# RWKV decays, rates and gates: computed for all head pairs when the mixing begins, as float32r products, and kept in DRAM

## The chip, the core and the metric

The kernel runs on one core of a Trainium2 chip (trn2). The metric is the device time of one execution in microseconds. A core has five engines that work beside one another: TensorE (PE; its weight loads are listed apart as PEld), VectorE (DVE), ScalarE (ACT), GpSimd (POOL) and SyncE (SP), whose queue issues nearly all DMAs here. Each engine works through its own list in order, and semaphores hold an instruction back until its inputs are there.

## What is computed

One step of a decoder layer for 512 prompt tokens and 8 x 8 sample tokens, 576 columns in all (`N`), between two SwiGLU feed-forward blocks. The middle of the layer, the mixing, has three branches (RWKV-7 time mixing, a convolution, a cross-attention), merged with gates. The change concerns these lines of the time mixing:

```
z = h @ p['w_in']
...
xm = zs + (prev - zs) * p['mu_shift']
...
r, k, v = xm[..., :c1], xm[..., c1:c2], xm[..., c2:c3]
wd, ad, gd = xm[..., c3:c4], xm[..., c4:c5], xm[..., c5:]      # widths 64, 64, 160
w_log = -jax.nn.softplus(-(p['w0'] + jnp.tanh(wd) @ p['w_decay_up'])) - 0.5
decay = jnp.exp(-jnp.exp(w_log))
a = jax.nn.sigmoid(p['a0'] + ad @ p['w_a_up'])
g = jax.nn.sigmoid(gd) @ p['w_g_up']
...
wkv_new, o = _wkv7_scan(wkv0, r_h, hd(decay), k_h, v_h, kk, kk * a_h)
...
y_a = (o.reshape(b, t, D_RWKV) * g) @ p['w_rwkv_out']
```

The decays, the rates `a` and the gates `g` have 512 channels each. They are low-rank products: 64, 64 and 160 inner channels.

## The kernel before

Channels lie on the 128 partitions and the 576 tokens in the columns, so a matrix product is a sequence of matmuls of 128 x 128 weights with 288 columns (`H`), for two halves. Large products are made in float32r: weight and operand are each split into a high part and a low part (`split`: ScalarE casts, VectorE subtracts), and three matmuls per block (high x high, high x low, low x high) are added up in PSUM (`mm3`). One projection of 128 outputs (`proj`) is 48 matmuls. Its 512 KB of weights come by DMA into one of two buffers `w` of pool `wp` (`wtile`, `wload`), and are split into the three buffers of pool `wq`. A buffer is given to the next load when its splits are done.

The mixing works on four pairs of heads (64 + 64 channels, j = 0 to 3). `lora` first makes the low-rank inputs with `shifted(12)`, `shifted(13)`, `shifted(14)`: a projection, then the token shift with `mu`. They stay in SBUF as `la` (tanh of the decay input, and the rate input) and `lg` (sigmoid of the gate input; its last 32 channels in `aux`). Then the steps of a plan written out by hand follow:

```
PLAN = ("A0 P0 I0 Y3 G0 J0 P1 B0 Y1 I1 X2 Y1 X2 J1 P2 B1 "
        "X1 I2 X2 C0 Y3 P3 J2 B2 X1 Z1 I3 Z3 J3 B3 Z2 L0 Z2")
```

A is the attention, P `prep` (operands of the chunks of pair j), I and J `inverse` and `joined` (a triangular inverse, with DMAs between), B `chain` (eight chunks in sequence, the samples, the norm and the gate of the pair), G and C the convolution, X, Y and Z output gates (projections that nothing in the pairs waits for), L the reload of the finished pairs. The order of the plan is a priority, not a fixed order: a scheduler puts each engine's list together when the program is built, by expected times, and takes later work forward where an engine would stand idle. Projections, gates and pair steps are therefore interleaved on TensorE.

In `prep` the decays and rates of a pair are products in plain float32 of `wda` (decay and rate weights, one below the other, each K = 64) with `la` (lines 805 and 819, through `full`, line 128), ScalarE applies the sigmoid, and the exponential gives `w`. In `chain` the gate is a float32 product of `wg` with `lg` (line 916, also through line 128), and VectorE multiplies the pair's result by it from PSUM (line 917).

SBUF is given out in pools that are opened and closed like a stack, from the left and from the right. When a pool comes to lie on bytes of a closed pool, all its tiles wait for every user of that pool. The first feed-forward block leaves on the left, from low to high: `x1`, `f1`, `h1`, `xe` (operands and, at its end, the memory tokens of the keys and values), `sp`. The mixing then puts `b1` and `lp` there, and, after `lora`, `b20`, `b21` and `b3`. The token-shift scratch pool `lz` lies on the right.

Of the kernel before, what the change touches and what calls it, by code (L numbers as in the profile page):

```python
# [46 lines left out]
def _q8(t, q):  # L47
    return t.rearrange("p (b q) -> p b q", q=q)


class _Builder:
# [9 lines left out]
    def par(self, name, i=0, rows=128):  # L61
        c = _COLS[name] + i
        return self.pv[:rows, c:c + 1]
# [48 lines left out]
    def proj(self, src, x, n=8, m=128):  # L112

        w = self.wload(src, n * m)
        ps = []
        for h in range(2):
            p = self.bank()[:m, :H]
            self.mm3(p, w, x, n, h, m)
            ps.append((slice(h * H, (h + 1) * H), p))
        return ps  # L120
# [47 lines left out]
    def build(self):  # L168
        tc, a = self.tc, self.a
        with ExitStack() as st:  # L170
# [14 lines left out]
            self.d_g0 = [dr.tile([128, N], F32, name=f"d_g0{i}") for i in range(8)]  # L185
            self.d_ya = [dr.tile([128, N], F32, name=f"d_ya{i}") for i in range(4)]

            s_mem = ExitStack()
# [376 lines left out]
    def shifted(self, m, out, zp):  # L565

        V, A = self.V, self.A
        rows = 32 if m == 14 else 128
        p = self.proj(self.a["w14"] if m == 14 else self.a["win"][m], self.xn, 8, rows)
# [14 lines left out]
    def lora(self, lp):  # L584
        A, a = self.A, self.a
        self.ssh = lp.tile([128, 15, NB], F32, name="ssh")
        self.sho = lp.tile([128, 15, 9], F32, name="sho")
        self.wda = lp.tile([128, 512], F32, name="wda")
        self.wg = [lp.tile([128, 512], F32, name="wg0"), lp.tile([128, 512], F32, name="wg1")[:32]]
        self.G.memset(self.sho[:, 14, :], 0.0)  # L590
        self.dma(self.ssh, a["ssh"])
        self.dma(self.wda, a["wda"])
        self.dma(self.wg[0], a["wg0"])
        self.dma(self.wg[1], a["wg1"])
        self.la = lp.tile([128, N], F32, name="la")
        aux = lp.tile([128, 600], F32, name="aux")
        self.lg = [lp.tile([128, N], F32, name="lg0"), aux[:32, :N]]
        self.t11 = aux[64:96, :N].rearrange("p (h c t) -> p h c t", h=2, c=9)
# [11 lines left out]
        for t in self.st + [self.ms, self.ax]:  # L610
            self.G.memset(t, 0.0)
        with self.tc.tile_pool(name="lz", bufs=1, side="right") as zp:
            self.shifted(12, self.la, zp)
            A.activation(self.la[:64], self.la[:64], AF.Tanh)
            for i in range(2):
                self.shifted(13 + i, self.lg[i], zp)
                A.activation(self.lg[i], self.lg[i], AF.Sigmoid)

# [172 lines left out]
    def prep(self, j):  # L791
# [6 lines left out]
        def parts(t, o=0):  # L798

            return _q8(t[:, :SEQ], 64), _q8(t[:, SEQ:N], 8)  # L800

        k, r, v = tmp("k"), tmp("r"), b2.tile([128, N], F32, name="v")

        sg = b1.tile([128, 640], F32, name="u1", bufs=2)[:, :N]
        for c, p in self.full("g", (self.wda[:64, 128 * j:128 * j + 128], self.la[:64])):
            A.activation(sg[:, c], p, AF.Sigmoid, bias=par("w0", j))
        w = b1.tile([128, PADN], F32, name="w")
        g = b1.tile([128, PADN], F32, name="g")
        for wv, sv in zip(self.padded(w), parts(sg)):
            V.memset(wv[:, :, 0:1], 0.0)  # L810
            A.activation(wv[:, :, 1:], sv, AF.Exp, scale=-0.6065306597126334)
        V.tensor_tensor_scan(g, w, self.gi, 0.0, ALU.mult, ALU.add)
# [5 lines left out]
        av = tmp("av")  # L818
        for c, p in self.full("g", (self.wda[64:, 128 * j:128 * j + 128], self.la[64:])):
            A.activation(av[:, c], p, AF.Sigmoid, bias=par("a0", j))  # L820

# [55 lines left out]
    def chain(self, j):  # L877
# [36 lines left out]
        V.tensor_tensor(rs, rs, bv, ALU.add)  # L914
        ch = slice(128 * j, 128 * j + 128)
        for c, p in self.full("c", (self.wg[0][:, ch], self.lg[0]), (self.wg[1][:, ch], self.lg[1])):
            V.tensor_tensor(rs[:, c], p, rs[:, c], ALU.mult)
        self.dbg(f"ya{j}", rs)
# [193 lines left out]
def _prep(inp):  # L1112
# [13 lines left out]
    def wt(w, cols=128):  # L1126

        K, M = w.shape
        return np.ascontiguousarray(
            w.reshape(K // 128, 128, M // cols, cols).transpose(2, 1, 0, 3).reshape(M // cols, 128, K // 128 * cols))  # L1130
# [14 lines left out]
    for i in "12":  # L1145
# [4 lines left out]
    a["win"] = wt(np.concatenate([win[:, :1792], win[:, 1824:]], axis=1))  # L1150
    a["w14"] = wt(win[:, 1792:1824], 32)[0]
    a["wya"] = wt(f["w_rwkv_out"])
    a["wcb"] = wt(f["w_conv_out"])
    a["woc"] = wt(f["w_xattn_out"])
    a["wo"] = wt(f["w_o"])
    a["wda"] = np.concatenate([f["w_decay_up"], f["w_a_up"]])
    a["wg0"] = np.ascontiguousarray(f["w_g_up"][:128])
    a["wg1"] = np.ascontiguousarray(f["w_g_up"][128:])
    cols = [vec(f["ffn1_norm"]), vec(f["mix_norm"]), vec(f["ffn2_norm"]), vec(f["final_norm"]), vec(f["mu_shift"])]
    cols += [vec(f[n].reshape(-1)) for n in ("w0", "a0", "k_k", "k_a", "r_k", "gn_g", "gn_b", "glu_b")]  # L1160
# [3 lines left out]
    a["ssh"] = np.ascontiguousarray(  # L1164
        np.concatenate([f["state_shift"], np.zeros((NB, 96), f["state_shift"].dtype)], axis=1)
        .reshape(NB, 15, 128).transpose(2, 1, 0))
# [63 lines left out]
```

## Time and profile before

| | us |
|---|---|
| median of three runs | 1486.97 (1484.86 to 1489.13) |
| the profiled execution | 1487.49 |
| its span, first to last instruction | 1485.7 |
| PE busy | 1460.2 |
| DVE busy | 1027.4 |
| ACT busy | 675.5 |
| mean granted TensorE clock | 0.982 |

How to read the rows of the profile: a group names line, engine and operation, output and inputs by the program's names (`p<-x,wh`), shapes, count; then the busy time of the group, the mean of one in ns, and the idle time of the engine just before them with what ended it. A row of the order of time begins with start and length in us. The rows of stretches give for each engine the busy time, then the granted TensorE clock, the DMA share and GB/s. A matmul's record is longer than the distance to the next one, since matmuls overlap in the array; the distance is what counts for throughput. L128 is the matmul in `full`, L110 that of `mm3k`, L96 and L97 the two halves of `split`, L86 the weight load.

### The profile page before, as it was taken

How to read it: one execution, taken by the hardware profiler on the slowest of the kernel's cores; microseconds unless marked ns; L12 is line 12 of the kernel's file. 1: busy time of each engine (PE TensorE's matmuls, PEld its weight loads, DVE VectorE, ACT ScalarE, POOL GpSimd, SP SyncE). 2: the span in 40 equal slices, each digit the busy share in tenths (PEclk: the TensorE clock that was granted, in tenths of full speed). 3: DMA queues.
4: the chain of work that ended last, by engine and by line, in shares of the span. 5: the costliest groups of instructions: out<-in, count | busy, mean ns of one | idle time of the engine just before them, and what ended most of it. 6: DMA issues, size and time to landing. Idle time of an engine off the chain costs nothing.

```text
span 1485.7 us, 27013 instructions
## 1 busy us (share of the span) xinstructions
PE 1460.2 (98%) x10778; PEld 1378.1 (93%) x10778; DVE 1027.4 (69%) x2053; ACT 675.5 (45%) x1370; POOL 4.5 (0%) x21
## 2 busy tenths in 40 slices
PE   8999999999999999999999999999999999999997
PEld 8999999999998799888889888789999999999997
DVE  7976777777784579778466456357578767777775
ACT  6443344443577535435446542444354434444342
POOL 0000000000010000000000000000000000000000
PEclk9999999999999999999899999999999999999998
DMA  6222222232632243133123134255222322322221
GB/s 209 72 84 87 86 86 86 86 98 95 205 101 86 66 132 91 46 98 96 60 65 97 55 100 126 92 177 175 100 72 72 100 73 85 102 95 89 86 86 64
DMA packets 95033, 144.04 MB, mean 97 GB/s; under 512 B 43628, under 2 KB 53228, under 8 KB 94908
## 3 DMA queue, kind: packets, MB, share of 16 engines
q1 hardware_dynamic: 94332, 141.74, 30.9%
q8 instruction: 84, 1.38, 0.4%
q10 hardware_dynamic: 576, 0.59, 0.1%
q14 instruction: 41, 0.34, 0.1%
HBM read 126.07 MB, written 16.23 MB: 96 GB/s over the span
## 4 chain that ended last, share of the span: by engine, by line
PE 92%; DVE 4%; ACT 2%; DMA 1%; issue 1%; SPq 0%; DVEq 0%; ACTq 0%
PE p L110 51%; PE p L369 26%; PE g L872 1%; PE c L1006 1%; PE c L1010 1%; PE c L1003 1%; DVE pr L965 1%; PE g L128 1%; PE c L128 1%; PE c L1038 1%; PE c L1036 1%; DMA w<-win 1%; PE p L148 1%; PE c L1021 1%; PE c L1058 1%
## 5 line engine op out<-in xcount | busy, mean ns | idle before, releaser
L110 PE MATMUL p<-x,wh 128*128 128x288 f32 x3136 | 655.4, 300 | 1.1 <-ACT kv L541 0.7
L110 PEld LDWEIGHTS p<-x,wh 128*128 128x128 f32 x3136 | 507.1, 188 | 15.2 <-issue 7.9
L110 PE MATMUL p<-x,wl 128*128 128x288 f32 x1568 | 469.7, 300 | 1.5 <-DVE wl L97 1.5
L96 ACT CAST wh<-w 128x512 fp32r<-128x512 f32 (+1 forms) x353 | 209.5, 600 | 257.2 <-PE p L110 111.9
L97 DVE TENSOR_TENSOR wl<-w,wh 128x512 fp32r<-128x512 f32 (+1 forms) x353 | 231.9, 662 | 109.2 <-ACT wh L96 102.2
L110 PEld LDWEIGHTS p<-x,wl 128*128 128x128 f32 x1568 | 295.2, 188 | 7.0 <-issue 3.1
L369 PE MATMUL p<-t,wh 128*128 128x288 f32 x1088 | 224.2, 298 | 0.0
L369 PEld LDWEIGHTS p<-t,wh 128*128 128x128 f32 x1088 | 173.8, 188 | 6.4 <-DVE t L380 6.2
L369 PE MATMUL p<-b,wh 128*128 128x288 f32 x816 | 169.7, 295 | 0.0
L369 PE MATMUL p<-t,wl 128*128 128x288 f32 x544 | 160.5, 295 | 0.0
L96 ACT CAST wh<-p 128x512 fp32r<-128x512 f32 x136 | 84.5, 621 | 155.9 <-PE p L110 117.7
L369 PEld LDWEIGHTS p<-b,wh 128*128 128x128 f32 x816 | 132.6, 188 | 0.0
L97 DVE TENSOR_TENSOR wl<-p,wh 128x512 fp32r<-128x512 f32 x136 | 93.5, 688 | 50.4 <-ACT wh L96 47.8
L369 PE MATMUL p<-b,wl 128*128 128x288 f32 x408 | 120.3, 295 | 0.0
L369 PEld LDWEIGHTS p<-t,wl 128*128 128x128 f32 x544 | 102.4, 188 | 0.0
L369 PEld LDWEIGHTS p<-b,wl 128*128 128x128 f32 x408 | 76.8, 188 | 0.0
L446 DVE SCALAR_TENSOR_TENSOR x<-p,x 128x288 f32<-128x288 f32 x128 | 57.7, 451 | 20.3 <-PE p L110 20.3
L96 ACT CAST x<-t 128x576 fp32r<-128x576 f32 (+1 forms) x60 | 36.5, 610 | 45.6 <-DVE t L450 42.3
L1030 DVE SCALAR_TENSOR_TENSOR st<-c,gc,mg 64x64 f32<-64x64 f32 x56 | 15.9, 283 | 53.3 <-PE c L1021 52.5
L359 DVE TENSOR_TENSOR p<-w 128x512 f32<-128x512 f32 x68 | 46.7, 686 | 3.2 <-DMA w<-wu 2.7
L359 DVE TENSOR_TENSOR p<-p,w 128x512 f32<-128x512 f32 x68 | 46.3, 681 | 0.1
L110 PE MATMUL p<-x,t 128*128 128x288 f32 x264 | 38.5, 306 | 5.5 <-ACT t L96 5.5
(345 smaller groups left out, 1987.8 us busy)
## 6 DMA issues: line engine op xcount, KB each, us to landing
w<-wu SPq DMA_DIRECT2D x85, 512.0 KB
w<-win SPq DMA_DIRECT2D x44, 512.0 KB
w<-wd SPq DMA_DIRECT2D x64, 256.0 KB
w<-wd SPq DMA_DIRECT2D x16, 384.0 KB
d_mb<-gate SPq DMA_DIRECT2D x16, 288.0 KB
w<-wo SPq DMA_DIRECT2D x8, 512.0 KB
x<-x SPq DMA_DIRECT2D x8, 288.0 KB
d_x<-x SPq DMA_DIRECT2D x16, 144.0 KB
```

Source lines behind the costliest of these rows:

```text
L96: self.A.copy(hi, x)
L97: self.V.tensor_tensor(lo, x, hi.bitcast(F32), ALU.subtract)
L110: self.T.matmul(p, l, x[r][:, c], start=k == 0 and i == 0, stop=k == n - 1 and i == 2)
L128: self.T.matmul(p, l, r[:, c], start=i == 0, stop=i == len(ops) - 1)
L148: self.T.matmul(p[:, o + f - d.start:o + 128 - d.start], r[f:, i], self.con("ident")[f:, f:], start=True, stop=True)
L359: V.tensor_tensor(s, u, v, ALU.add)
L369: self.T.matmul(p, hl[l][:, c], xs[k][b][:, o], start=first and k == 0 and q == 0, stop=k == 3 and q == 2, skip_group_check=True)
L446: V.scalar_tensor_tensor(x[m][:, c], p, 0.5, x[m][:, c], ALU.mult, ALU.add)
L872: T.matmul(ps[:, i * 128:(i + 1) * 128], kb[o, c + i].rearrange("p a t -> p (a t)"), ra[o, c + i].rearrange("p a t -> p (a t)"), start=Tru ...
L965: V.tensor_tensor(pr, tt[:, :n, :e].unsqueeze(2).broadcast_to([np_, n, m, e]), l3[:, t:e, :e].unsqueeze(1).broadcast_to([np_, n, m, e]), A ...
L1003: T.matmul(ps[64:, 64 * h:64 * h + 64], gr[:64, h, c, 64:], vu[:64, c, 64 * h:64 * h + 64], start=h == 0 or not inter, stop=not inter)
L1030: V.scalar_tensor_tensor(mn[s, s], ps[s, 256 + 64 * h:320 + 64 * h], gc[s, c:c + 1], mg[s, s], ALU.mult, ALU.add)
```

## The change

A new function, `low_rank`, takes the place of the three calls at the end of `lora`. It loads the decay and rate weights stacked twice (`wda`, now 128 x 1024) and the gate weights (`wg`, 128 x 1024, the last 32 rows three times) through the two buffers `w`, splits them, and makes the inputs as before, split too. High and low parts are stacked on the partitions so that a decay or rate product takes two float32r matmuls for a half, and a gate product four. Sigmoid and exponential follow for all four pairs, and `w`, `a` and the gates go to DRAM (`d_w`, `d_a`, `d_gt`). `prep` and `chain` load them back. `shifted(14)` now makes 96 rows (its 32 channels three times), and the scratch pool `lz` is on the left, above `lp`, and also holds the split weights and inputs.

```diff
     def proj(self, src, x, n=8, m=128):
-        w = self.wload(src, n * m)
+        w = self.wload(src, n * m, 512 // m * m)
...
     def shifted(self, m, out, zp):
-        rows = 32 if m == 14 else 128
+        rows = 96 if m == 14 else 128
...
     def lora(self, lp):
-        self.wda = lp.tile([128, 512], F32, name="wda")
-        self.wg = [lp.tile([128, 512], F32, name="wg0"), lp.tile([128, 512], F32, name="wg1")[:32]]
...
-        with self.tc.tile_pool(name="lz", bufs=1, side="right") as zp:
-            self.shifted(12, self.la, zp)
-            A.activation(self.la[:64], self.la[:64], AF.Tanh)
-            for i in range(2):
-                self.shifted(13 + i, self.lg[i], zp)
-                A.activation(self.lg[i], self.lg[i], AF.Sigmoid)
+        with self.tc.tile_pool(name="lz", bufs=1) as zp:
+            self.low_rank(zp)
+
+    def low_rank(self, zp):
+        two = lambda name, n: zp.tile([128, 2, n], F32R, name=name)
+        sub = lambda o, x, hi: V.tensor_tensor(o, x, hi.bitcast(F32), ALU.subtract)
+        wh, wl, gh, gl = two("wh", 512), zp.tile([128, 512], F32R, name="wl"), two("gh", 512), zp.tile(
+            [128, 512], F32R, name="gl")
+        xs, lg, gs = two("xs", N), two("lg", N), zp.tile([128, N], F32R, name="gs")
+        raw = []
+        for name in ("wda", "wg"):
+            raw.append(self.wtile())
+            self.dma(raw[-1], a[name])
+        raw = [t.rearrange("p (i c) -> p i c", i=2) for t in raw]
+        A.copy(wh, raw[0])
+        for i in range(2):
+            o = slice(64 * i, 64 * i + 64)
+            sub(wl[o], raw[0][o, i], wh[o, i])
+        A.copy(gh, raw[1])
+        sub(gl, raw[1][:, 0], gh[:, 0])
+        sub(gh[64:96, 1], raw[1][64:96, 1], gh[64:96, 1])
+
+        x = b1.tile([128, N], F32, name="k")
+        self.shifted(12, x, b1)
+        A.activation(x[:64], x[:64], AF.Tanh)
+        for i in range(2):
+            o, q = slice(64 * i, 64 * i + 64), slice(64 - 64 * i, 128 - 64 * i)
+            A.copy(xs[o, i], x[o])
+            sub(xs[q, i], x[o], xs[o, i])
+        x = b1.tile([128, N], F32, name="r")
+        self.shifted(13, x, b1)
+        A.activation(x, x, AF.Sigmoid)
+        self.split(lg[:, 0], lg[:, 1], x)
+        x = b1.tile([128, N], F32, name="av")[:96]
+        self.shifted(14, x, b1)
+        A.activation(x, x, AF.Sigmoid)
+        A.copy(gs[:96], x)
+        sub(gs[32:64], x[32:64], gs[32:64])
+
+        def products(*ops):
+            for h in range(2):
+                c = slice(h * H, (h + 1) * H)
+                p = self.bank("g")[:, :H]
+                for q, (l, r) in enumerate(ops):
+                    T.matmul(p, l, r[:, c], start=q == 0, stop=q == len(ops) - 1)
+                yield c, p
+
+        sg = [b1.tile([128, 640], F32, name="u1", bufs=2)[:, :N] for _ in range(2)]
+        sg += [b1.tile([128, N], F32, name="bv", bufs=2) for _ in range(2)]
+        for j in range(4):
+            ch = slice(128 * j, 128 * j + 128)
+            for c, p in products((wh[:, 0, ch], xs[:, 0]), (wl[:64, ch], xs[:64, 0])):
+                A.activation(sg[j][:, c], p, AF.Sigmoid, bias=self.par("w0", j))
+            t = b1.tile([128, N], F32, name=("k", "r")[j % 2])
+            for c, p in products((wh[:, 1, ch], xs[:, 1]), (wl[64:, ch], xs[64:, 1])):
+                A.activation(t[:, c], p, AF.Sigmoid, bias=self.par("a0", j))
+            self.store(self.d_a[j], t)
+        for j in range(4):
+            ch = slice(128 * j, 128 * j + 128)
+            t = b1.tile([128, N], F32, name=("av", "zt")[j % 2])
+            for c, p in products((gh[:, 0, ch], lg[:, 0]), (gh[:, 0, ch], lg[:, 1]), (gl[:, ch], lg[:, 0]),
+                                 (gh[:96, 1, ch], gs[:96])):
+                A.copy(t[:, c], p)
+            self.store(self.d_gt[j], t)
+        for j in range(4):
+            w = b1.tile([128, PADN], F32, name=("w", "g")[j % 2])
+            for wv, sv in zip(self.padded(w), (_q8(sg[j][:, :SEQ], 64), _q8(sg[j][:, SEQ:], 8))):
+                V.memset(wv[:, :, 0:1], 0.0)
+                A.activation(wv[:, :, 1:], sv, AF.Exp, scale=-0.6065306597126334)
+            self.store(self.d_w[j], w)
...
     def prep(self, j):
-        for c, p in self.full("g", (self.wda[:64, 128 * j:128 * j + 128], self.la[:64])):
-            A.activation(sg[:, c], p, AF.Sigmoid, bias=par("w0", j))
...
-        for wv, sv in zip(self.padded(w), parts(sg)):
-            V.memset(wv[:, :, 0:1], 0.0)
-            A.activation(wv[:, :, 1:], sv, AF.Exp, scale=-0.6065306597126334)
+        self.dma(w, self.d_w[j])
...
-        for c, p in self.full("g", (self.wda[64:, 128 * j:128 * j + 128], self.la[64:])):
-            A.activation(av[:, c], p, AF.Sigmoid, bias=par("a0", j))
+        self.dma(av, self.d_a[j])
...
     def chain(self, j):
-        for c, p in self.full("c", (self.wg[0][:, ch], self.lg[0]), (self.wg[1][:, ch], self.lg[1])):
-            V.tensor_tensor(rs[:, c], p, rs[:, c], ALU.mult)
+        gt = b3.tile([128, N], F32, name="gt")
+        self.dma(gt, self.d_gt[j])
+        V.tensor_tensor(rs, gt, rs, ALU.mult)
```

The host side stacks the weights, `mu_shift` and the shift state accordingly.

More of the change, by code (lines that the diff above doesn't have):

```diff
@@ L186, in build @@
             self.d_ya = [dr.tile([128, N], F32, name=f"d_ya{i}") for i in range(4)]
+            self.d_w = [dr.tile([128, PADN], F32, name=f"d_w{i}") for i in range(4)]
+            self.d_a = [dr.tile([128, N], F32, name=f"d_a{i}") for i in range(4)]
+            self.d_gt = [dr.tile([128, N], F32, name=f"d_gt{i}") for i in range(4)]
             s_mem = ExitStack()
@@ L584, in lora @@
     def lora(self, lp):
-        A, a = self.A, self.a
+        a = self.a
         self.ssh = lp.tile([128, 15, NB], F32, name="ssh")
         self.sho = lp.tile([128, 15, 9], F32, name="sho")
-        self.wda = lp.tile([128, 512], F32, name="wda")
-        self.wg = [lp.tile([128, 512], F32, name="wg0"), lp.tile([128, 512], F32, name="wg1")[:32]]
         self.G.memset(self.sho[:, 14, :], 0.0)
         self.dma(self.ssh, a["ssh"])
[L592 to L595, printed above, removed]
         aux = lp.tile([128, 600], F32, name="aux")
-        self.lg = [lp.tile([128, N], F32, name="lg0"), aux[:32, :N]]
         self.t11 = aux[64:96, :N].rearrange("p (h c t) -> p h c t", h=2, c=9)
@@ L611, in lora @@
             self.G.memset(t, 0.0)
-        with self.tc.tile_pool(name="lz", bufs=1, side="right") as zp:
-            self.shifted(12, self.la, zp)
-            A.activation(self.la[:64], self.la[:64], AF.Tanh)
-            for i in range(2):
-                self.shifted(13 + i, self.lg[i], zp)
-                A.activation(self.lg[i], self.lg[i], AF.Sigmoid)
+        with self.tc.tile_pool(name="lz", bufs=1) as zp:
+            self.low_rank(zp)
+    def low_rank(self, zp):
+        V, A, T, a, b1 = self.V, self.A, self.T, self.a, self.b1
+        two = lambda name, n: zp.tile([128, 2, n], F32R, name=name)
[61 more added lines that the diff above has]
+            self.store(self.d_w[j], w)
@@ L802, in prep @@
         k, r, v = tmp("k"), tmp("r"), b2.tile([128, N], F32, name="v")
-        sg = b1.tile([128, 640], F32, name="u1", bufs=2)[:, :N]
-        for c, p in self.full("g", (self.wda[:64, 128 * j:128 * j + 128], self.la[:64])):
-            A.activation(sg[:, c], p, AF.Sigmoid, bias=par("w0", j))
         w = b1.tile([128, PADN], F32, name="w")
         g = b1.tile([128, PADN], F32, name="g")
-        for wv, sv in zip(self.padded(w), parts(sg)):
-            V.memset(wv[:, :, 0:1], 0.0)
-            A.activation(wv[:, :, 1:], sv, AF.Exp, scale=-0.6065306597126334)
+        self.dma(w, self.d_w[j])
         V.tensor_tensor_scan(g, w, self.gi, 0.0, ALU.mult, ALU.add)
@@ L914, in chain @@
         V.tensor_tensor(rs, rs, bv, ALU.add)
-        ch = slice(128 * j, 128 * j + 128)
-        for c, p in self.full("c", (self.wg[0][:, ch], self.lg[0]), (self.wg[1][:, ch], self.lg[1])):
-            V.tensor_tensor(rs[:, c], p, rs[:, c], ALU.mult)
+        gt = b3.tile([128, N], F32, name="gt")
+        self.dma(gt, self.d_gt[j])
+        V.tensor_tensor(rs, gt, rs, ALU.mult)
         self.dbg(f"ya{j}", rs)
@@ L1150, in _prep @@
     a["win"] = wt(np.concatenate([win[:, :1792], win[:, 1824:]], axis=1))
-    a["w14"] = wt(win[:, 1792:1824], 32)[0]
+    a["w14"] = wt(np.concatenate([win[:, 1792:1824]] * 3, axis=1), 96)[0]
     a["wya"] = wt(f["w_rwkv_out"])
@@ L1155, in _prep @@
     a["wo"] = wt(f["w_o"])
[L1156 to L1159, printed above, removed]
+    a["wda"] = np.concatenate([np.concatenate([f[n]] * 2) for n in ("w_decay_up", "w_a_up")], axis=1)
+    g = f["w_g_up"]
+    a["wg"] = np.concatenate([g[:128], np.concatenate([g[128:]] * 3 + [np.zeros_like(g[128:])])], axis=1)
+    cols = [vec(f["ffn1_norm"]), vec(f["mix_norm"]), vec(f["ffn2_norm"]), vec(f["final_norm"]), vec(np.concatenate([f["mu_shift"]] + [f["mu_shift"][-32:]] * 2))]
     cols += [vec(f[n].reshape(-1)) for n in ("w0", "a0", "k_k", "k_a", "r_k", "gn_g", "gn_b", "glu_b")]
@@ L1164, in _prep @@
     a["ssh"] = np.ascontiguousarray(
-        np.concatenate([f["state_shift"], np.zeros((NB, 96), f["state_shift"].dtype)], axis=1)
+        np.concatenate([f["state_shift"]] + [f["state_shift"][:, -32:]] * 2 + [np.zeros((NB, 32), np.float32)], axis=1)
         .reshape(NB, 15, 128).transpose(2, 1, 0))
```

## The prediction

> **What bounds the kernel now.** I read the page first (busy times, chain), then the stretches of the mixing stage, then the groups by line for the instructions that go, and at last the order of time around 422 us, where the change puts its new work.
>
> ```profile
> PE 1460.2 (98%) x10778; PEld 1378.1 (93%) x10778; DVE 1027.4 (69%) x2053; ACT 675.5 (45%) x1370; POOL 4.5 (0%) x21
> ...
> PE 92%; DVE 4%; ACT 2%; DMA 1%; issue 1%; SPq 0%; DVEq 0%; ACTq 0%
> ```
>
> TensorE carries 92% of the chain that ends last. That is an average, so here are the stretches of the mixing stage (about 423 to 993 us), all that the change touches.
>
> ```profile
> core 0: us, PE busy (x) PEld busy (x) DVE busy (x) ACT busy (x) POOL busy (x), PEclk, DMA share, GB/s
> 423.00:455.00 32.00, 32.00 (x241) 30.86 (x242) 23.00 (x74) 20.91 (x49) 3.55 (x15) 1.00 0.56 165
> 455.00:480.00 25.00, 24.97 (x166) 21.59 (x165) 11.58 (x20) 20.94 (x50) 0.00 (x0) 1.00 0.13 43
> 660.00:720.00 60.00, 57.71 (x444) 54.54 (x444) 50.60 (x105) 26.59 (x58) 0.00 (x0) 0.94 0.30 89
> 900.00:993.00 93.00, 88.99 (x652) 76.18 (x650) 41.39 (x84) 36.62 (x88) 0.00 (x0) 0.93 0.43 130
> ```
>
> TensorE is full everywhere but in 660 to 720 us (2.3 us idle, VectorE at 50.6 of 60) and 900 to 993 us (4.0 us idle). A microsecond taken from TensorE is therefore worth nearly one, except in the stretch that VectorE shares; a microsecond in which TensorE is kept without work costs one in full.
>
> **What goes.** The groups by line and shape, and pieces of the chain in order of time (start, us, what):
>
> ```profile
> L128 PE MATMUL g<-la,wda 64*128 64x288 f32 x32 | 9.4, 442 | 0.5 <-ACT u L806 0.5
> L128 PE MATMUL c<-aux,wg 32*128 32x288 f32 x16 | 6.0, 453 | 0.0
> L128 PE MATMUL c<-lg,wg 128*128 128x288 f32 x16 | 5.9, 452 | 0.0
> ```
>
> ```profile
> 455.78 1.16 PE g L128 x4
> 657.83 2.72 PE c L128 x8
> 993.20 89.31 PE p L110 x671
> ```
>
> Each float32 product appears as two records, so x32 is 16 products. One L128 pair of halves for decays or rates holds TensorE 1.16 us (455.78), a pair's four gate products 2.72 us (657.83). Removed: 8 x 1.16 = 9.3 us (two for each of four head pairs), and 4 x 2.72 = 10.9 us, together 20.2 us. A float32r matmul of the same 288 columns runs at 89.31 / 671 = 0.133 us. The change issues, for each pair, 4 for the decays, 4 for the rates and 8 for the gates: 64 x 0.133 = 8.5 us. Net of the arithmetic: -11.7 us.
>
> The Trainium skill (FP8 and Floating Point Precision, TensorE Precision Notes) says that true float32 makes 4 passes through the array. By that, 32 products would be 32 x 4 x 0.133 = 17.0 us, and the sum at the end would be 3.2 us higher; the rows above have the duration itself (20.2 us), so they are used.
>
> **What comes, at 422 us.** Projection weights pass through two buffers `w`. Now the first two loads of the mixing are those of projections 12 and 13, issued long before; the splits are done in time and TensorE starts 0.69 us after the last matmul of the stage before.
>
> ```profile
> 395.03 0.37 SPq L86 DMA_DIRECT2D w<-win  x1
> 398.14 0.38 SPq L86 DMA_DIRECT2D w<-win  x1
> 422.00 0.28 PE L110 MATMUL p<-wh,t 128*128 128x256 f32 x1
> 422.96 0.53 PE L110 MATMUL p<-x,wh 128*128 128x288 f32 x2 [0.69 <-ACT kv L541]
> 422.34 0.95 POOL L549 MEMSET kT<- 128x1024 f32 x1 [421.48 <-PE p L110]
> 428.49 0.10 POOL L590 MEMSET sho<- 128x9 f32 x1 [5.08 <-DVE x L97]
> ```
>
> After the change these two buffers are taken first by the raw `wda` and `wg` (512 KB each). They come free only when ScalarE has made `wh`/`gh` from them and VectorE the low parts. Those targets lie in pool `lz`, 23.8 KB a partition, on bytes that the first FFN's pools `h1` and `xe` held; the two POOL rows show that a new pool waits for the last user of the old (`kT` for the matmul of 422.00, `sho` for the last split of 427.61). So the copy can't start before 422.3, the load of projection 12 waits for it, and TensorE has no other matmul: every projection needs a `w` buffer.
>
> ```profile
> 423.15 0.62 ACT L553 COPY vm<-kv 128x512 f32<-128x512 f32 x1
> 423.67 1.25 ACT L552 COPY kT<-kv 64x512 f32<-64x512 f32 x2
> 427.61 0.82 DVE L97 TENSOR_TENSOR x<-t,x 128x288 fp32r<-128x288 f32 x2
> 428.56 0.68 DVE L97 TENSOR_TENSOR wl<-w,wh 128x512 fp32r<-128x512 f32 x1
> 435.43 1.14 ACT L96 CAST wh<-w 128x512 fp32r<-128x512 f32 x2
> 571.59 8.04 DMA w<-win
> 920.00 3.01 DMA aux<-s
> ```
>
> Prices: the copy of 1024 columns 1.14 us (435.43, two of 512), two subtractions 2 x 0.68, then the load, then the cast 0.6 and the low part 0.7 of the projection's own weights. The load lies between a small DMA on an idle queue (3.01) and a 512 KB weight load among other transfers (8.04); I take 4.0, nearer the small one, since little else is on the queue then. Lower end: all at once from 422.3: 1.1 + 1.4 + 3.0 + 1.3 = 6.8, start 429.1, a delay of 6.1 us against 422.96. Upper end: ScalarE first does `vm`, `kT` and the stage's own casts, VectorE first ends the norm (428.4): 428.4 + 1.4 + 8.0 + 1.3 = 439.1, a delay of 16.1 us. I take 10: both engines serve the older work first, so the subtractions end at about 428 (VectorE has two projection splits of 0.68 less in its way there), and 428 + 4.0 + 1.3 = 433.3. On VectorE the norm's last splits stand behind a subtraction that waits for `wh`; they too are needed only at 433. An array left idle also loses clock:
>
> ```profile
> 923.00:926.00 3.00, 2.02 (x48) 1.91 (x49) 0.42 (x1) 1.24 (x4) 0.00 (x0) 0.79 0.67 225
> 926.00:930.00 4.00, 4.00 (x35) 3.72 (x33) 0.69 (x2) 2.29 (x5) 0.00 (x0) 0.50 0.14 33
> 1083.00:1086.00 3.00, 1.69 (x12) 1.60 (x12) 0.95 (x3) 1.64 (x3) 0.00 (x0) 0.86 0.08 25
> 1086.00:1090.00 4.00, 4.00 (x21) 3.66 (x21) 2.52 (x6) 2.77 (x4) 0.00 (x0) 0.67 0.30 113
> ```
>
> The granted clock (the column before the DMA share) fell after gaps: 0.21 x 3 + 0.50 x 4 = 2.6 us lost behind the gap at 921, 0.14 x 3 + 0.33 x 4 = 1.7 us behind that at 1083. The second is followed by dense 288-column matmuls, as here, so 1.7; ends 0 and 2.6. The Trainium skill (TensorE: Matmul & The Clock Gate, Part 1) gives half rate until about 3.4 us of sustained work have passed, which is an estimate of 1.7 us lost whatever the gap. By it the sum stays as it is; by the row at 923 it would be 0.9 us higher; no row shows a gap of 10 us.
>
> **Beside other work.** In the new function ScalarE gets the two big copies (2 x 1.14), about 2.7 us of operand copies, 16 sigmoids and the exponentials (moved from the pairs) and 8 gate copies, some 19 us in a stretch where it had 20.9 busy of 32:
>
> ```profile
> L820 ACT ACTIVATE av<-g,pv 128x288 f32<-128x288 f32 x8 | 4.0, 501 | 0.1
> L806 ACT ACTIVATE u<-g,pv 128x288 f32<-128x288 f32 x8 | 4.0, 502 | 2.5 <-PE g L128 2.5
> L820 ACT ACT_TABLE_LOAD x4 | 5.1, 1283 | 0.1
> L917 DVE TENSOR_TENSOR u<-c,u 128x288 f32<-128x288 f32 x8 | 3.4, 456 | 0.1
> ```
>
> Two products (0.27 us) feed a sigmoid of 0.50, so the products run at ScalarE's pace; what covers TensorE are projections 13, 14 and the two of the attention (4 x 48 x 0.133 = 25.5 us). If that cover fails, the cost is the difference, 16 x 0.24 = 3.8 us, kept in the upper end. VectorE gets eight subtractions of 0.68 to 0.75 (5.8 us) where it had 9 us free; per pair its two L917 from PSUM (0.91) become one of 576 columns (about 0.74). Twelve stores and twelve loads of about 290 KB join the SP queue (0.33 us of issue each): a store that waits for its product holds back the weight load queued behind it. The loads of `w`, `av`, `gt` in the pairs can go out well before their use; I cost them nothing, with the projections of the same pair as cover, and a round of 3.0 us or more for each pair without it. Projection 14 with 96 instead of 32 rows has the same 48 matmuls and two casts as before (480 and 288 columns instead of 512 and 256); its 384 KB load has two projections of cover. Zero for each. In the pairs, the 0.5 us that TensorE idled for L806 goes.
>
> **Sum.** +10 (start) +1.7 (clock) +8.5 (products) -20.2 (removed) -0.5 (L806) = -0.5. Of the removed, about 5 us (the gates at 657.83 and the decays and rates of the third pair) lie beside the stretch where VectorE is at 50.6 of 60; they may be worth 0 to 5, and I take half: +2.5. Total +2.0 us. The profiled run took 1487.49 us (span 1485.7), 0.5 above the median of 1486.97; from the median I forecast **1489 us**, no change that can be told (0.3% is 4.5 us; the bounds are 1482.5 and 1491.4). Low ends together: 6.1 + 0 + 8.5 - 20.2 - 0.5 = -6.1 us; high ends: 16.1 + 2.6 + 8.5 + 3.8 + 5 - 20.2 = +15.8.
>
> **Rivals.** (1) *The start is not lost.* If the raw parts are through before 422, or the first projection gets its buffer ahead of them, the 11.7 us go and the rest stays: 1489 - 11.7 = 1477.3. For it: both raw loads can be in at about 400. Against it: the POOL rows. Its half (start delayed 6.1 us, clock kept) gives 1483.4. (2) *Slower: the SP queue.* At about 445 to 475 us the stores wait for products that ScalarE delivers late, and weight loads stand behind them. With two buffers a load can be at most one projection ahead, 48 x 0.133 = 6.4 us, and needs 4.0 + 1.3; so it decides from a hold of 1.1 us. Four gate stores held 2 us past that cost 8 us: 1497. For it: ScalarE at 20.9 of 32 before 19 us are added. Against: the order of the queue is laid out by expected times, and 455 to 480 us has a DMA share of 0.13. (3) *Slower: the pairs' own chains bind.* If the pair steps keep their pace (solve, state, inverse) and TensorE only idles more, about half of the 17.9 us taken out after the first pair is not had: 1489 + 9 - 2.5 = 1495.5. For it: 900 to 993 us idles 4.0 us, part of it behind the inverse's last DMA (920.00). Against: only 6.3 us of idle in the two worst stretches now.
>
> **How the numbers follow.** Forecast 0.42 (its own range 1483 to 1495), rival 1 0.24, rival 2 0.18, rival 3 0.16. Faster by over 4.5 us: rival 1 and 0.03 of the forecast, 0.27. Slower: rivals 2 and 3 and 0.03 of the forecast, less 0.01: 0.36. Same: 0.37. The range runs from 1478 (half of rival 1 below) to 1501 (the tails of 2 and 3 above).
>
> **What the next profile would show.** TensorE idle from 422.3 to about 433 and then a few us at a clock under 1; the first cast of projection 12 released by a DMA; no L128 under `la`, `lg` or `aux`; 64 matmuls of about 0.133 us spacing in their place before 480; pairs without their L811 and L820 table loads. I am wrong if TensorE starts by 425 (then 1477), if it idles between 445 and 480 behind a weight load, or if its idle time after 600 us grows by more than 5 us.

## The result and the profile after

The changed kernel took 1526.12 us (median of 6 runs, 1521.83 to 1531.5), the kernel before 1484.94 us on the same chip (6 runs, 1484.25 to 1489.13). The ratio is 1.0274, 95% interval 1.0253 to 1.0296: 41 us slower, far outside the forecast's range.

The page of the changed kernel, busy times and chain:

```profile
PE 1478.9 (97%) x10778; PEld 1398.4 (91%) x10778; DVE 1030.8 (67%) x2058; ACT 689.0 (45%) x1391; POOL 4.5 (0%) x21
...
PE 88%; DVE 5%; ACT 3%; DMA 2%; issue 1%; SPq 0%; DVEq 0%; ACTq 0%
```

TensorE has lost four points of the chain; VectorE, ScalarE and DMA have one more each. Three matmuls mark the stages: the first of the attention (`c<-kT,q`), the first Gram matrix of the first pair (`g<-ra,kb`, the products inside a chunk from which the triangular inverse starts) and the first of the merge (`p<-k`). TensorE's order of time, first before, then after (in the second also the first matmul of projection 12):

```profile
454.76 1.02 PE L708 MATMUL c<-kT,q 128*128 128x512 f32 x2
...
496.40 0.49 PE L872 MATMUL g<-ra,kb 64*128 64x128 f32 x2
...
993.20 0.40 PE L110 MATMUL p<-k,wh 128*128 128x288 f32 x1 [0.62 <-DVE gate L783]
```

```profile
434.34 0.85 PE L110 MATMUL p<-x,wh 128*128 128x288 f32 x2 [11.23 <-ACT wh L96]
...
497.91 1.02 PE L772 MATMUL c<-kT,q 128*128 128x512 f32 x2
...
539.53 0.49 PE L930 MATMUL g<-ra,kb 64*128 64x128 f32 x2
...
1035.10 0.40 PE L110 MATMUL p<-k,wh 128*128 128x288 f32 x1 [0.62 <-DVE gate L847]
```

The attention starts 43.1 us later, the first Gram matrix 43.1 us later, the merge 41.9 us later. The profiled execution was the longest of the six (1531.5 us, 44.0 more than the profiled one before), so the 43.1 are to be read against 44.0, not against the 41 of the medians. Nearly all of the loss lies ahead of 498 us, and the pairs gave back 1.2 us: from the first Gram matrix to the merge 496.8 us before and 495.6 after. The pairs had 17.9 us of float32 products less in that stretch. Both stretches by windows, before and after:

```profile
423.00:500.00 77.00, 76.41 (x527) 67.58 (x528) 49.80 (x132) 55.58 (x140) 3.55 (x15) 1.00 0.32 96
500.00:993.00 493.00, 484.96 (x3564) 420.13 (x3562) 303.50 (x672) 226.42 (x518) 0.00 (x0) 0.96 0.31 92
```

```profile
423.00:540.00 117.00, 97.28 (x584) 83.70 (x583) 59.75 (x151) 86.60 (x193) 4.15 (x15) 0.87 0.34 110
540.00:1035.00 495.00, 481.64 (x3509) 424.02 (x3508) 298.11 (x660) 211.37 (x490) 0.00 (x0) 0.93 0.31 91
```

In the second row of each, the idle time of TensorE went from 8.0 to 13.4 us and the granted clock from 0.96 to 0.93, and 0.03 of 495 us is 15 us: the work that was taken out came back as 5 us of idle and a lower clock.

Ahead of that there are two stalls. The first is the forecast one, here in the order of time of all engines:

```profile
426.49 1.04 ACT L626 CAST wh<-w 128x1024 fp32r<-128x1024 f32 x1
...
429.02 0.69 DVE L617 TENSOR_TENSOR wl<-w,wh 64x512 fp32r<-64x512 f32 x1
...
429.74 1.78 SPq L86 DMA_DIRECT2D w<-win  x2
...
433.67 1.14 ACT L96 CAST wh<-w 128x512 fp32r<-128x512 f32 x2 [0.91 <-DMA w<-win]
```

The second was not foreseen. ScalarE in the order of time:

```profile
471.33 1.28 ACT L664 ACT_TABLE_LOAD   x1
472.62 0.89 ACT L664 ACTIVATE bv<-g,pv 128x288 f32<-128x288 f32 x2
473.53 1.28 ACT L680 ACT_TABLE_LOAD   x1
474.83 0.26 ACT L680 ACTIVATE g<-u 128x64 f32<-128x64 f32 x1
475.10 1.28 ACT L667 ACT_TABLE_LOAD   x1
476.39 0.89 ACT L667 ACTIVATE k<-g,pv 128x288 f32<-128x288 f32 x2
```

The sigmoids of decays (L664) and rates (L667) alternate with the exponentials of the decays (L680), although the program has all exponentials last; the scheduler pulled each forward to where its input was ready. Sigmoid and exponential need different tables, so nearly every step pays a load of 1.28 us: 13 of them start from 458.63 to 485.22 us, where one would do. TensorE works in order and stands behind those sigmoids. Its waits from 420 to 500 us (who for whom, total, times, longest), and its clock:

```profile
PE p L110 <- ACT wh L96: 11.2, 1, 11.2
PE g L656 <- ACT bv L664: 4.7, 2, 2.8
PE g L656 <- ACT r L667: 1.9, 2, 1.6
PE g L656 <- ACT k L667: 1.6, 1, 1.6
```

```profile
460.00:480.00 20.00, 14.49 (x66) 10.40 (x65) 0.94 (x5) 18.56 (x25) 0.00 (x0) 0.81 0.19 75
480.00:500.00 20.00, 17.02 (x84) 15.12 (x85) 8.12 (x7) 14.64 (x34) 0.00 (x0) 0.68 0.48 165
```

ScalarE is busy 18.56 of 20 us while TensorE gets 66 matmuls through (150 at 0.133 us each), and the clock falls to 0.81 and 0.68.

### The profile page after: what moved, and what is told of

Its sections match the earlier page's. It is cut to its first block, busy times and chain, and to the rows that moved or that the text cites. A ratio compares the mean times of both kernels' runs of the same rounds, so it can differ in the third digit from the quotient of the medians.

```text
span 1529.7 us, 27100 instructions
## 1 busy us (share of the span) xinstructions
PE 1478.9 (97%) x10778; PEld 1398.4 (91%) x10778; DVE 1030.8 (67%) x2058; ACT 689.0 (45%) x1391; POOL 4.5 (0%) x21
## 4 chain that ended last, share of the span: by engine, by line
PE 88%; DVE 5%; ACT 3%; DMA 2%; issue 1%; SPq 0%; DVEq 0%; ACTq 0%
PE p L110 49%; PE p L372 25%; PE c L1064 1%; PE g L930 1%; DMA w<-win 1%; PE c L1068 1%; PE c L1061 1%; DVE pr L1023 1%; PE c L1096 1%; DVE cc L719 1%; PE c L1094 1%; PE c L962 1%; PE c L825 1%; PE c L1116 1%; PE g L656 1%
## 5 line engine op out<-in xcount | busy, mean ns | idle before, releaser
L110 PE MATMUL p<-x,wh 128*128 128x288 f32 x3136 | 666.4, 304 | 14.9 <-ACT wh L96 14.4
L110 PEld LDWEIGHTS p<-x,wh 128*128 128x128 f32 x3136 | 517.8, 193 | 25.4 <-ACT wh L96 15.3
L110 PE MATMUL p<-x,wl 128*128 128x288 f32 x1568 | 474.6, 304 | 1.7 <-DVE wl L97 1.6
L110 PEld LDWEIGHTS p<-x,wl 128*128 128x128 f32 x1568 | 300.8, 192 | 7.8 <-DVE wl L97 2.7
```

The costliest lines, as they stand in the source:

```text
L110: self.T.matmul(p, l, x[r][:, c], start=k == 0 and i == 0, stop=k == n - 1 and i == 2)
```

## The experiments

### Three stalls taken away

**The exponentials behind the last sigmoid** (exp_last).

```diff
-                A.activation(t[:, c], p, AF.Sigmoid, bias=self.par("a0", j))
+                last = A.activation(t[:, c], p, AF.Sigmoid, bias=self.par("a0", j))
...
+                with self.tc.issue_after(last.ins):
                     A.activation(wv[:, :, 1:], sv, AF.Exp, scale=-0.6065306597126334)
```

> The changed kernel with one edit: the exponentials of the four decays (L680) are queued on ScalarE behind the last sigmoid of the rates (L667). In the changed kernel's trace they stand between the sigmoids, and 13 table loads of 1.28 us lie between 458.63 and 485.22 us. Theory A (the tables hold TensorE up, because each product's bank is freed by a sigmoid that waits for its table): 12 of the 13 loads go, 15.4 us, and the clock in 460 to 500 rises again from 0.81 and 0.68, which by the 20 x (1 - clock) sums is worth up to 8 us more; 1526 - 15.4 = 1511, down to 1503. The L656 products' idle behind L664 and L667, 17.7 us in the changed kernel, falls under 5. Rival B (the late start and the round trip through DRAM set the time; ScalarE's tables lie beside it): 1526 +/- 3, and the first scan stays at 492.

Ratio 1.0159 (1.0131 to 1.0187): 1.15% or 17 us less than the changed kernel, with some 5 us of uncertainty either way, between the 15.4 of the loads alone and the 23 with the clock. One table load is left for the exponentials, and L656 waits for nothing any more. (The 17.7 us of the expectation count each wait twice, for the matmul and for its weight load; TensorE itself waited the 8.2 us listed above.) The same windows read:

```profile
460.00:480.00 20.00, 20.00 (x116) 16.29 (x117) 2.25 (x7) 15.28 (x36) 0.00 (x0) 1.00 0.47 173
480.00:500.00 20.00, 18.87 (x129) 16.49 (x128) 12.07 (x19) 12.59 (x40) 0.00 (x0) 1.00 0.34 116
```

Theory A holds and rival B falls: the table loads are the largest single cause.

**The weights behind projection 13** (weights_first). The block that loads and splits `wda` and `wg` moves below `self.shifted(13, x, b1)`.

> The changed kernel with one edit: the loads of the decay, rate and gate weights and the arithmetic that splits them (L620 to L632) are moved behind projection 13, so that the first two tiles of the weight buffers go to projections 12 and 13 as before the change. Theory A (the start is lost to the two buffers): the first projection starts near 423 instead of 434.3, and all of it is kept, since the table loads follow at a fixed distance: 1526 - 11.4 = 1514.7, within 1512 to 1518. Rival C (the split weights now come too late for the products, and the start comes back as a wait there): 1524 to 1529.

Ratio 1.0197 (1.0158 to 1.0235), 11.4 us less than the changed kernel, with some 7 us of uncertainty either way. Projection 12 starts at 423.37 us again, so the start was lost as forecast. That it counts in full isn't shown: the products now wait 2.4 us for the split activation, the clock stands at 0.53 from 440 to 450 us, and the attention starts 8.0 us earlier than in the changed kernel, not 11. Rival C is right in part.

**Both edits** (both).

> The changed kernel with both edits, exponentials behind the sigmoids and weights behind projection 13. Theory A (tables 15.4 and more, start 11.4, both on TensorE's path and additive): 1526 - 15.4 - 11.4 = 1499, down to 1491 with the clock. What is then left over the kernel before (1485) is 6 to 14 us: 8.5 of the new products and what the clock still loses, while the 20.2 us of products that the pairs no longer have must then be worth nearly nothing. If they were worth their 20.2 once the two stalls are gone, it would come out near 1473 to 1480.

Ratio 1.0076 (1.0051 to 1.0101): 29.4 us less than the changed kernel, where the two single edits sum to 28.5. Within these intervals they add. What was left in the stretch, waits and clock:

```profile
PE g L656 <- DVE xs L617: 2.3, 1, 2.3
PE p L110 <- DVE wl L97: 0.8, 1, 0.8
```

```profile
440.00:449.00 9.00, 9.00 (x30) 0.50 0.41 149
```

A wait of 2.3 us stands ahead of these 9 us at half clock: 4.5 us lost on top of the gap itself.

**The weights in tiles of their own** (own_tiles), so that projections 12 to 14 keep both weight buffers. The exponentials stay behind the last sigmoid, here and in all further edits of the changed kernel:

```diff
-        for name in ("wda", "wg"):
-            raw.append(self.wtile())
-            self.dma(raw[-1], a[name])
+        for name, tag, n in (("wda", "u1", 640), ("wg", "bv", N)):
+            for i in range(2):
+                raw.append(b1.tile([128, n], F32, name=tag, bufs=2)[:, :512])
+                self.dma(raw[-1], a[name][:, 512 * i:512 * i + 512])
```

> The changed kernel with the exponentials behind the sigmoids (as in exp_last), and with the weights of decays, rates and gates loaded into four tiles that the pairs use later (u1 and bv, 512 columns each) in place of the two tiles of the weight buffers, so that projections 12, 13 and 14 find both buffers free and the split weights are there when the products come. In the kernel with both edits (ratio 1.0076) one gap was left: the products waited 2.27 us for the split activation at 439.2, and the clock stood at 0.50 from 440 to 448.8. Theory A (every gap costs itself and 5 us of clock behind it): the gap goes and 6 to 8 us with it; ratio 1.002 to 1.004, 1490 to 1493. Rival (the loads come late through the one queue, the products wait and the gap only moves): ratio 1.007 to 1.010.

Ratio 1.0108 (1.0073 to 1.0144): no gain, a miss. The long gap and the half clock did go (the attention starts at 473.0 against 477.9 in the kernel with both edits, the first Gram matrix at 514.9 against 517.2), but from there to the first matmul of the merge it took longer (495.9 against 489.4 us); see the order, below. The profiled run was also the longest of its four (1507.97 us, median 1501.15).

**Full rows** (full_rows). What stayed was the products' own spacing. TensorE's order of time in the kernel with late gates (below), which has the same products:

```profile
452.68 0.29 PE L659 MATMUL g<-xs,wh 128*128 128x288 f32 x1
452.91 0.39 PE L659 MATMUL g<-xs,wl 64*128 64x288 f32 x1
453.23 0.40 PE L659 MATMUL g<-xs,wh 128*128 128x288 f32 x1
453.56 0.39 PE L659 MATMUL g<-xs,wl 64*128 64x288 f32 x1
```

From start to start 0.23 to 0.33 us at full clock, where 0.133 was priced. The edit puts zeros beside the low parts, so that the second product has 128 rows:

```diff
-        wh, wl, ... = two("wh", 512), zp.tile([128, 512], F32R, name="wl"), ...
+        wh, wl, ... = two("wh", 512), two("wl", 512), ...
...
-            for c, p in products((wh[:, 0, ch], xs[:, 0]), (wl[:64, ch], xs[:64, 0])):
+            for c, p in products((wh[:, 0, ch], xs[:, 0]), (wl[:, 0, ch], xs[:, 0])):
```

> The kernel own_tiles (ratio 1.0108) with one edit: the low parts of the decay and rate weights stand in tiles of all 128 rows with zeros in the unused half, so that the second product of each bank has 128 rows in place of 64; the products' values are unchanged. In the kernel with late gates a product with all rows and the following one with 64 rows take 0.22 + 0.33 us from start to start at full clock, where two products of the projections take 0.27. Theory A (a change between 128 and 64 rows costs TensorE the overlap of the weight load): 16 pairs x 0.28 = 4.5 us less, ratio 1.008 from 1.0108, and the start-to-start time falls to 0.133. Rival (the spacing comes from the banks that ScalarE empties): spacing as before, within 2 us of own_tiles.

Ratio 1.0045 (1.0027 to 1.0063), and the spacing is gone:

```profile
457.53 0.30 PE L659 MATMUL g<-xs,wh 128*128 128x288 f32 x1
457.67 0.29 PE L659 MATMUL g<-xs,wl 128*128 128x288 f32 x1
457.79 0.43 PE L110 MATMUL p<-x,wh 128*128 128x288 f32 x2
```

The step from own_tiles is 9.4 us, with some 6 us of uncertainty either way; the spacing accounts for 4.5. In the trace the attention starts at 468.53 us in place of 473.04, 4.5 us earlier. So the mechanism and its size are shown ahead of the attention; in the total the size is shown only roughly. With three stalls mended, 6.7 of the 41 us are left.

### The products that came

**No products** (own_tiles_no_products): own_tiles with the products left out; the sigmoids and the gate copies read the split activation from SBUF.

> The kernel own_tiles with the 64 float32r products left out: the sigmoids read the split activation from SBUF and the gates are copied from it, so decays, rates and gates are not the products; loads, splits, stores and reloads stay. It asks what the new products cost where they stand. Theory A (they lie uncovered ahead of the first pair's Gram matrices): 64 x 0.133 = 8.5 us less than own_tiles. Rival (TensorE has gaps there that hide them): within 2 us of own_tiles. That the pairs have lost their 20.2 us of products and this kernel has none at all makes it, if TensorE's work counted in full, 20.2 us faster than the kernel before: 1466; if the pairs' own chains set the pace, near 1482 to 1486.

Ratio 1.0084 (1.0069 to 1.0099), 3.6 us less than own_tiles, between the two theories and settling neither. A new wait had opened where the products had been:

```profile
459.65 0.85 PE L110 MATMUL p<-x,wh 128*128 128x288 f32 x2 [14.54 <-ACT wh L96]
```

The cast of the next projection's weights stood in ScalarE's order behind the moved sigmoids, gate copies and exponentials, from 445 to 459 us without a pause. The products had covered that.

**Late gates** (late_gates): the gates' 32 products emitted behind the first pair's preparation. To make room, the attention's cached keys have two buffers in place of three, and the pools of the later pairs are opened after that preparation.

> The kernel own_tiles with the gates' 32 products issued behind the first pair's preparation in place of ahead of the attention (their parts stay in SBUF until then, for which one of three buffers of the attention's cached keys is given up). Theory A (what stands ahead of the first Gram matrices counts, what stands behind them is hidden): 32 x 0.133 = 4.3 us less than own_tiles. Rival (the attention loses more to its two buffers, or the products fall into a place where the pair waits for them): the same or slower than own_tiles.

Ratio 1.008 (1.0058 to 1.0102), 4.2 us less than own_tiles as theory A has it, but the two intervals overlap, so it is not shown.

**Late gates with full rows (late_full), and then with the weights behind projection 13 (late_full_raw13).**

> late_gates (ratio 1.008) with the full rows of full_rows. Theory A (the 64 rows cost 4.5 us ahead of the first Gram matrices, in full): ratio 1.005, 1493. Rival: as late_gates, 1.008.

> late_full with the four loads of the decay, rate and gate weights and their splitting emitted behind projection 13. In late_gates TensorE waited 1.87 us at 439.96 for the weights of projection 14, whose load stands beside the 1 MB of these four loads. Theory A (the four loads delay projection 14's weights): the gap goes and 2 to 4 us with it, ratio 1.002 to 1.004; that is the kernel before within what can be told. Rival (the split weights come too late for the products, and the gap moves there): 1.005 to 1.007.

1.0147 (1.0132 to 1.0162) and 1.005 (1.0034 to 1.0066). The first is a clear miss: 10 us slower than late_gates for an edit that saves TensorE time, and moving four loads takes it back. The saving itself arrived: the attention starts at 463.71 us, in late_gates at 467.73. The time went behind it: from the first Gram matrix to the merge late_full took 504.2 us, late_full_raw13 492.9. Their windows from 500 to 1000 us, first late_full, then late_full_raw13:

```profile
500.00:1000.00 500.00, 484.17 (x3511) 0.93 0.31 92
```

```profile
500.00:1000.00 500.00, 483.61 (x3602) 0.96 0.33 97
```

Nearly the same busy time, but 91 matmuls fewer and a clock of 0.93 against 0.96. The two have the same number of matmuls, in another order.

**Full rows with the weights behind projection 13** (full_rows_raw13).

> full_rows (ratio 1.0045) with the four loads of the decay, rate and gate weights and their splitting emitted behind projection 13, so that the weights of projections 13 and 14 don't stand behind 1 MB of them. In full_rows TensorE waits 1.55 us at 440.3 and 1.62 us at 448.2. Expected: 2 to 3 us of this go, ratio 1.002 to 1.004; if the split weights then come too late, 1.004 to 1.007. Faster than the kernel before is not expected: 8.5 us of products still stand uncovered ahead of the first Gram matrices, against some 5 us of the first pair's that went.

Ratio 1.0054 (1.0034 to 1.0073): no better than full_rows. No version of the change came out faster than the kernel before.

### The products that went

In these kernels the expectations give the first pair's decays and rates as 4.6 us; by the rows of the prediction they are 2 x 1.16 = 2.3, so that 17.9 us lie behind the first Gram matrices, not 15.6.

**All left out, in the kernel before** (before_no_products; `p` replaced by the activation in SBUF):

> The kernel before with the float32 products of the pairs left out and nothing put in their place: the sigmoids of decays and rates (L806, L820) read the low-rank activation from SBUF, and the gate's multiplication (L915) reads the gates' activation; the up-projections of decay, rate and gate are not computed. It asks what the 20.2 us of TensorE work are worth where they stood. If TensorE is the bound through the pairs: 1485 - 20.2 = 1465. If the pairs are bound by their own chains and TensorE's work there stands in gaps: 1483 to 1485. The changed kernel suggests the second: from the first attention product to the merge's first matmul it takes 537.2 us against 538.4.

Ratio 1.0041 (1.0023 to 1.006): slower, by neither theory. The order had changed, and a gap of 4.57 us with a low clock behind it had opened ahead of the attention:

```profile
454.85 0.61 PE L110 MATMUL p<-x,wl 128*128 128x288 f32 x1 [4.57 <-DVE wl L97]
```

**Issued twice** (before_double; `*[...] * 2` around the operands of `full`):

> The kernel before with each float32 product of the pairs (L128, 64 matmuls) issued twice into the same accumulation: decays, rates and gates get twice the product. It puts 20.2 us of TensorE work more into the pairs, where before_no_products took 20.2 us away and gained nothing (ratio 1.0041). If the pairs' chains have room beside them: at most 4.6 us, the first pair's eight matmuls ahead of its Gram matrices, ratio 1.000 to 1.004. If TensorE's work counts when it is added although it doesn't when it is taken away (the pairs stand at the balance): 10 to 20 us, ratio 1.007 to 1.014.

Ratio 1.0146 (1.0117 to 1.0176): 21.7 us (17 to 26) for 20.2 us of work. Added work counts in full or nearly so.

**Only those behind the first Gram matrices left out, then the gates alone, then decays and rates of pairs 1 to 3 alone:**

> The kernel before with the float32 products left out that stand behind the first Gram matrices: the decays and rates of pairs 1 to 3 and the gates of all four pairs, 20.2 - 4.6 = 15.6 us of TensorE work; the first pair's decays and rates stay, since leaving those out opened a gap of 4.57 us at 455 with the clock at 0.50 behind it. Those outputs are then not the products. Theory A (behind the first Gram matrices the pairs' own chains set the pace, and work that is taken away comes back as idle and low clock): ratio 0.998 to 1.001. Rival (the 8 us that before_no_products lost at 455 hid a gain): 15.6 us less or a good part of it, ratio 0.990 to 0.994.

> The kernel before with the gates' float32 products of all four pairs left out (4 x 2.72 = 10.9 us of TensorE); the multiplication reads the gates' activation, so the gates are not the products. before_no_late_products (these and the decays and rates of pairs 1 to 3) measured 0.9941, 8.8 us of 15.6. Theory W (the worth follows the work, a bit over half of it): 6 us, ratio 0.996. Theory C (a chain's end counts in full, and the gates stand at each pair's end, the last one ahead of the merge): 8 to 11 us, ratio 0.993 to 0.995. Theory O (the order decides, by chance): anything between 0.990 and 1.005, not adding up with before_no_rates.

> The kernel before with the float32 products of decays and rates of pairs 1 to 3 left out (6 x 1.16 = 7.0 us, less than 15.6 - 10.9 = 4.7 if the first pair's weigh more); those outputs are then not the products. Theory W: 3 to 4 us, ratio 0.997 to 0.998. Theory C (they stand ahead of the pairs' preparation, beside the pair before): nothing, 0.999 to 1.001. Theory O: anything between 0.990 and 1.005, not adding up with before_no_gates to 0.9941.

0.9941 (0.9929 to 0.9953), 0.9948 (0.9925 to 0.9971) and 0.9981 (0.9962 to 1.0): 8.8 of 17.9 us, 7.7 of 10.9, 2.8 of 7.0. The two parts sum to 10.5, within the intervals of the 8.8. So my theory of chains that set the pace whatever TensorE does fell; the removed work came out worth about half. That the gates are worth more than decays and rates isn't shown: the intervals are some 3 us either way on each. Leaving products out changes the order of the rest too, so the 8.8 us are work and order together.

**The order alone** (before_fill_swapped). One step of the plan is moved, with not an instruction more or less:

```diff
-PLAN = ("A0 P0 I0 Y3 G0 J0 P1 B0 Y1 I1 X2 Y1 X2 J1 P2 B1 "
+PLAN = ("A0 P0 I0 Y3 G0 J0 P1 B0 Y1 I1 X2 X2 Y1 J1 P2 B1 "
```

> The kernel before with one step of the plan moved: of the work that fills the first pair's inverse, the gate projection Y1 is emitted behind the two gated products X2 in place of between them. Not an instruction more or less; the order of TensorE differs from about 40% of the program on. It asks what a change of order alone does. Theory W or C: within 0.3% of the kernel before, 0.997 to 1.003. Theory O: 0.4% or more off, to either side.

Ratio 1.0076 (1.0053 to 1.0099): 11 us slower. The window from 500 to 1000 us, first the kernel before, then this one:

```profile
500.00:1000.00 500.00, 491.76 (x3615) 0.96 0.32 93
```

```profile
500.00:1000.00 500.00, 490.15 (x3559) 0.95 0.30 88
```

An order of the same work moves the time by about as much as the products that went are worth. From the first Gram matrix to the merge it took 504.9 us against 496.8: 2.4 us of it are idle time (10.7 against 8.3), 5.1 are clock (51.2 us at half clock against 41.0). Most of such a loss thus lies in time in which TensorE is called busy. How, can be seen in the kernel before itself, five microseconds a row:

```profile
710.00:715.00 5.00, 5.00 (x60) 1.00 0.30 108
715.00:720.00 5.00, 5.00 (x56) 0.66 0.11 26
720.00:725.00 5.00, 5.00 (x24) 0.50 0.07 13
725.00:730.00 5.00, 5.00 (x33) 0.82 0.30 76
```

No idle time is shown, yet the clock falls to 0.50 for some 10 us and the matmuls per row to about half.

The kept traces show what goes ahead of such a fall. In all 18 of them the clock is either full or half, and a stretch at half clock lasts 3.41 us or a multiple of it. I cut each trace into steps on this grid, count the columns of the matmuls that start in a step, and compare with a dense stream, 288 columns every 0.133 us. Of the steps at full clock that had less than 0.32 of a dense stream, all 131 were followed by a step at half clock; of those with 0.5 or more, none of 6953; of those between, 83 of 405. In the stretch above, the step from 713.1 us had 0.42; the step with the wait of 2.3 us in the kernel with both edits had 0.23; the two waits of 1.6 us in full_rows left 0.47 and 0.51, and the clock stayed. So TensorE need not stand idle: a few microseconds of few columns are enough. This is read from the traces; no run varied the columns and nothing else, and what decides between 0.32 and 0.5 is open.

## Why the prediction was wrong, step by step

**Start, +10: right.** TensorE started at 434.34 against 422.96, 11.4 us, by the rows named: subtraction until 429.7, load 3.9 (4.0 taken), cast 0.6. In the kernel with the weights behind projection 13 TensorE starts 11.0 us earlier again.

**Clock after the gap, +1.7: right there, missed elsewhere.** These windows of the changed kernel show 0.50 until about 438:

```profile
428.00:434.00 6.00, 0.00 (x0) 0.00 (x0) 3.17 (x10) 2.17 (x6) 2.61 (x11) 0.50 0.98 303
434.00:438.00 4.00, 3.66 (x14) 3.44 (x15) 2.33 (x5) 1.42 (x3) 0.00 (x0) 0.50 0.93 185
438.00:440.00 2.00, 2.00 (x17) 2.00 (x16) 2.00 (x12) 0.36 (x1) 0.00 (x0) 0.97 0.72 225
```

From 434.3 to 438 that is half of 3.7 us, 1.8. The Trainium skill (TensorE: Matmul & The Clock Gate, Part 1) gives half rate after an idle window of about 3.4 us and release after about 3.4 us of sustained work; this gap agrees. The 9 us at 0.50 behind a wait of 2.3 us, in the kernel with both edits, do not.

**Products at ScalarE's pace, covered: this step failed, and it cost most.** The pace was taken as 0.50 us for each sigmoid, the cost without cover as 3.8 us. The rows of the table loads (1283 ns each) were quoted, but only as loads that the pairs would lose; I took the program's order, in which all exponentials come last, for the order on the engine. The loads, with the clock behind them, cost some 17 us. The cover named (projections 13, 14 and the attention's) was there, but an in-order TensorE can't go past a product whose bank waits. The Trainium skill (ScalarE: Activation LUTs, What ACT_TABLE_LOAD costs) gives about 2.66 us for a change of tables, a load of 1283 ns and a drain of 1380 ns. The load agrees; no drain is seen here, since the sigmoid at 472.62 starts 0.01 us after its load ends, and the load 0.02 us after the exponential before it.

**64 products, +8.5: too small.** Half of them alternate between 128 and 64 rows and take 0.55 us a pair and more, not 0.27: 4.5 us on top.

**Removed, -20.2: the second step that failed.** 2.3 us stood ahead of the first Gram matrices and went; the 17.9 us behind them changed Gram-to-merge by 1.2 us. Left out of the kernel before they are worth 8.8 us, and in the changed kernel even these didn't show: TensorE's idle time there grew by 5.2 us and its time at half clock from 41.0 to 71.7 us. With stalls mended, part of them does: the same stretch took 491.8 us in exp_last, 489.4 with both edits and 487.0 in full_rows, but 495.9 in own_tiles. "A microsecond taken from TensorE is therefore worth nearly one" was read from busy shares of 96 to 100%, which hide the clock and the spacing of small matmuls. The discount of 2.5 us should have been some 9 by the run that left them out.

**The sum again, to the first Gram matrix.** 11.4 (start) + 1.8 (clock) + 8.5 - 2.3 (products) + 4.5 (64 rows) + 8.5 (L656's waits, those of the list and 0.3 more) + 6.9 (from 472.9 to 492.4 us the clock stood at 0.50 and TensorE was busy for 13.85 us, of which half is lost; its idle time there is among the waits already) = 39.3, where 43.1 was measured. The other 3.8 us are unexplained.

**The rivals.** (1), the start not lost, is excluded by the 11.23 us. (2), a slower kernel through ScalarE's delay, had the place and the sign right but the wrong carrier: the waits are for sigmoids, none for a weight load between 440 and 500 us. (3), the pairs' pace, is half right: the mark was 5 us more idle time after 600 us, and it grew from 17.9 to 23.9 us, or to 22.0 if it is counted from the same point of the program on. But most of what the pairs lost is clock, which the sign named didn't cover.

**What stays open.** The falls of the clock in the pairs follow steps of few columns; why one order has more of these than another wasn't settled. Nor was the last 6.7 us: ahead of the first Gram matrix full_rows is 14.7 us late, of which 8.5 - 2.3 are products and 3.6 further waits; the other 5 are unexplained, and 9.8 are won back by the merge.

## What to carry to other kernels

Before moving activations of two kinds into one place, ask in which order the scheduler will put them: a change of tables was 1.28 us here, and everything that waits for the same engine pays it. A small gap on TensorE costs more than itself when the clock falls behind it (2.3 us did, 1.6 us did not), and work that is taken from a 98% busy engine may come back as clock and idle time; read the columns per window and the clock beside the busy share. Before a gain of under 1% is put down to an edit, try the same work in another order.

## What the runs showed of the hardware

A matmul of 64 rows among matmuls of 128 rows of the same size spaced its neighbours at 0.23 to 0.33 us instead of 0.133; one of 96 rows did not (full_rows):

```profile
458.72 0.29 PE L659 MATMUL g<-lg,gl 128*128 128x288 f32 x1
458.85 0.30 PE L659 MATMUL g<-gs,gh 96*128 96x288 f32 x1
458.98 0.29 PE L659 MATMUL g<-lg,gh 128*128 128x288 f32 x1
```

That a wait of 2.3 us was followed by 9 us at half clock, and that the clock halves in stretches without idle time, behind steps of few columns, was also new to me.
